# Input projections by one level of Strassen's identity, with output projections in a phase of their own

## The chip, the cores and the metric

One core of one Trainium2 chip runs the whole inference step in one launch. The metric is device microseconds of that core. The core has five engines with their own instruction streams: TensorE (PE) for matmuls, VectorE (DVE), ScalarE (ACT), GpSimd (POOL) and SyncE (SP); DMA transfers are issued from SP's, ACT's and POOL's queues. Matmuls read from on-chip memory (SBUF, 128 partitions) and write to PSUM, which has eight banks of 128 x 512 fp32 numbers.

## The reference

Two decoder layers on 1024 prompt rows and 64 sample rows (8 sequences of 8), all fp32. Layer 0 mixes with a gated short convolution, layer 1 with differential attention; a SwiGLU feed-forward follows each.

```python
D_MODEL, SEQ, D_FF, ALPHA = 1024, 1024, 2816, 4 ** 0.25
gb, gc, h = split(x @ w_conv_in, 3)               # layer 0, w_conv_in 1024 x 3072
u = gc * h                                        # with two rows of state ahead of it
conv = taps[0]*u[s] + taps[1]*u[s+1] + taps[2]*u[s+2]
m = (gb * conv) @ w_conv_out                      # 1024 x 1024
...                                               # layer 1: q, k, v = x @ w_qkv; rope; attention
m = attention_rows @ w_attn_out                   # 1024 x 1024
x = layernorm(ALPHA * x + m)                      # both layers, rows of prompt and samples alike
gate, up = split(x @ w_ffn_in, 2)                 # 1024 x 5632
x = layernorm(ALPHA * x + (silu(gate) * up) @ w_ffn_out)   # 2816 x 1024
```

## The kernel before

Every fp32 operand of a large matmul is split into a high and a low part (`split_to`, L74: ACT copies to the rounded type, DVE subtracts), and a product is three passes, high x high, high x low and low x high (`passes`, L87). The activations stand transposed in SBUF, features on partitions: `xTh` and `xTl`, eight blocks of 128 x 1088 columns (64 sample rows, then 1024 prompt rows).

*Input projections* (`in_type`, L98). One feature tile is 128 columns of a weight matrix. Its weights are loaded (`load_split`, one DMA of 512 KB and one split of 128x1024), and for each of three column chunks (364, 362, 362) 8 x 3 matmuls accumulate in one PSUM bank, which a callback consumes: for the convolution a copy or a product by the gate, for the feed-forward a Silu (L367) or a product (L372), whose result is split at once into `hh` and `hl`, the stationary operands of the output projection.

*Output projections* (`out_type`, L117) are mixed into the input projections: `run_chunks` makes two features (or 1, 3, 4 at the ends), then adds their part of the output to all eight row tiles of the residual stream, which stays in SBUF (`st`). For a row tile and a half of the columns 3 matmuls of 512 columns per feature accumulate in one bank, and DVE adds the bank to the stream (`residual`, L115). Sample rows take fp32 matmuls of their own (L125). In the last of these chunks each row tile gets its layer norm (`ln_prompt`, L151) and, two tiles later, its transposes into `xTh` and `xTl` (`to_xT`, L211), while other row tiles are still being multiplied.

*Attention* (layer 1) projects q, k and v in pieces of 256 columns (L687), with paged sample attention interleaved; its normalised heads are transposed and split into `xTh` and `xTl` by `place` (L803). The stream waits in DRAM (`x2_dram`) meanwhile.

The order of instructions on each engine is set by a planner that takes, of those it believes ready, the one that stands first in the program; within `manual_schedule` blocks an engine keeps the program's order. Each engine then runs its instructions in that order.

```python
wsp = ...tile_pool(name="wsp", bufs=9)            # split weights, 4 KB a partition each
pout, pin: 4 + 4 PSUM banks                       # output sums, input sums
run_chunks(pout, st, (2,) * 9 + (4,), feature, i_["wfo"][layer], ln)
```

Of the kernel before, what the change touches and what calls it, by code (L numbers as in the profile page):

```python
# [18 lines left out]
P = 128  # L19
# [5 lines left out]
CH = ((0, 364), (364, 362), (726, 362))  # L25
# [4 lines left out]
DS = 8  # L30
# [7 lines left out]
LAM_INIT = 0.8 - 0.6 * math.exp(-0.3)  # L38


class Ring:
    def __init__(self, *pools):
        self.pools = cycle(pools)

    def tile(self, *args, **kw):
        return next(self.pools).tile(*args, **kw)
# [3 lines left out]
def decoder_kernel(ctx: ExitStack, tc: tile.TileContext, i_: dict, o_: dict):  # L50
# [5 lines left out]
    wsp = ctx.enter_context(tc.tile_pool(name="wsp", bufs=9))  # L56
# [4 lines left out]
    xTh = cst.tile([P, KT, NT], F32R, name="xTh")  # L61
    xTl = cst.tile([P, KT, NT], F32R, name="xTl")
    mhalf = cst.tile([P, 1], F32, name="mhalf")
    POOL.memset(mhalf, -0.5)

    q_dram = drp.tile([NP, D], F32, name="q_dram")
    x2_dram = drp.tile([NP, D], F32, name="x2_dram")
    s2_dram = drp.tile([P, 512], F32, name="s2_dram")
    pairs = cst.tile([P, P], F32, name="pairs")
# [28 lines left out]
    def in_type(pin, src, consume, chunks=CH):  # L98
        wh, wl, _ = src if isinstance(src, tuple) else load_split(src)
        for c0, cw in chunks:  # L100
            ps = pin.tile([P, 512], F32, name="pin", tag="pin")
            for k in range(KT):
                for n, (a, b) in enumerate(passes(wh, wl, xTh, xTl)):
                    PE.matmul(  # L104
                        ps[:, :cw], a[:, k * P:(k + 1) * P], b[:, k, c0:c0 + cw],
                        start=(k == 0 and n == 0), stop=(k == KT - 1 and n == 2),
                    )
            consume(c0, cw, ps[:, :cw])

    def residual(a, ps, first, s):  # L110
        if first or s is not None:
            kw = {} if s is None else {"accum_out": s}
            DVE.scalar_tensor_tensor(a, a, ALPHA if first else 1.0, ps, op0=ALU.mult, op1=ALU.add, **kw)
        else:
            DVE.tensor_tensor(a, a, ps, op=ALU.add)  # L115

    def out_type(pout, st, acts, wts, first, ln=None, at=0):  # L117
        last = len(acts) - 1

        def sample():  # L120
            ss = sml.tile([P, 1], F32, name="lsms", tag="lsms", bufs=2) if ln else None
            ps = pout.tile([P, 512], F32, name="pouts", tag="pout")
            for j, ((_, _, hs), (_, _, raw)) in enumerate(zip(acts, wts)):
                for half in range(2):
                    PE.matmul(ps[half * NS:half * NS + NS, :], hs, raw[:, half * 512:half * 512 + 512],  # L125
                              start=(j == 0), stop=(j == last), skip_group_check=True)
            residual(st["s"], ps, first, ss)
            return ln_sample(pout, st, ss, ln) if ln else iter(())

        for t in range(8):  # L130
            if t == at:
                side = sample()
            t0 = NS + t * P
            s = sml.tile([P, 2], F32, name="lsm", tag="lsm") if ln else None
            for hf in range(2):
                ps = pout.tile([P, 512], F32, name="pout", tag="pout")
                cs = slice(hf * 512, hf * 512 + 512)
                for j, ((ah, al, _), (wh, wl, _)) in enumerate(zip(acts, wts)):
                    for n, (a, b) in enumerate(passes(ah, al, wh, wl)):
                        PE.matmul(ps, a[:, t0:t0 + P], b[:, cs],  # L140
                                  start=(j == 0 and n == 0), stop=(j == last and n == 2))
                residual(st[t][:, cs], ps, first, None if s is None else s[:, hf:hf + 1])
            if ln:
                ln_prompt(st, t, s, ln)
                next(side, None)
                if t >= 2 and ln["turn"]:
                    to_xT(pout, st[t - 2], t - 2)
        if ln and ln["turn"]:
            to_xT(pout, st[6], 6)
            to_xT(pout, st[7], 7)  # L150

    def ln_prompt(st, t, s, ln):
        x = st[t]
        g, b = ln["gb"]
        nmu = sml.tile([P, 1], F32, name="nmu", tag="nmu")
        DVE.tensor_scalar(nmu, s[:, 0:1], s[:, 1:2], -1.0 / D, op0=ALU.add, op1=ALU.mult)
        junk = ln["pool"].tile([P, D], F32, name="junk", tag="gb", bufs=1)
        ss = sml.tile([P, 1], F32, name="lss", tag="lss")
        ACT.activation(junk, x, AF.Square, bias=nmu[:, 0:1], accum_out=ss)
        r = rstd_of(ss, 1.0 / D, EPS)  # L160
        if t == 7 and not ln["turn"]:
            y = st[0]
            DVE.scalar_tensor_tensor(y, x, nmu[:, 0:1], g, op0=ALU.add, op1=ALU.mult)
            for eng, cs in ((SP, slice(0, 512)), (ACT, slice(512, D))):
                DVE.scalar_tensor_tensor(y[:, cs], y[:, cs], r[:, 0:1], b[:, cs], op0=ALU.mult, op1=ALU.add)
                eng.dma_start(ln["keep"][t * P:t * P + P, cs], y[:, cs])
            return
        DVE.scalar_tensor_tensor(x, x, nmu[:, 0:1], g, op0=ALU.add, op1=ALU.mult)
        DVE.scalar_tensor_tensor(x, x, r[:, 0:1], b, op0=ALU.mult, op1=ALU.add)
        if ln["keep"] is not None:  # L170
            SP.dma_start(ln["keep"][t * P:t * P + P, :], x)

    def ln_sample(pout, st, s, ln):
        x = st["s"]
# [7 lines left out]
        ps = pout.tile([P, 1], F32, name="pln", tag="pout")  # L182
        PE.matmul(ps, pairs, s, start=True, stop=True)
        nmu = sml.tile([P, 1], F32, name="nmus", tag="nmus", bufs=2)
        DVE.tensor_scalar(nmu, ps, -1.0 / D, None, op0=ALU.mult)
        junk = ln["pool"].tile([P, D], F32, name="junk", tag="gb", bufs=1)
        ss = sml.tile([P, 1], F32, name="lsss", tag="lsss", bufs=2)
        ACT.activation(junk[:, :512], x, AF.Square, bias=nmu[:, 0:1], accum_out=ss)
        yield
        ps = pout.tile([P, 1], F32, name="pln", tag="pout")  # L190
        PE.matmul(ps, pairs, ss, start=True, stop=True)
        t = sml.tile([P, 1], F32, name="lts", tag="lts", bufs=2)
        DVE.tensor_copy(t, ps)
# [6 lines left out]
        ln["keeps"](x)  # L200
        if ln["turn"]:
            ps = pout.tile([P, 4, 2, NS], F32, name="ptrs", tag="pout")
            for j in range(4):
                PE.transpose(ps[:, j, :, :].rearrange("p h t -> p (h t)"), x[:, j * P:j * P + P], ident)
            hi, lo = (y[:, :, 0:NS].rearrange("p (h j) t -> p j h t", j=4) for y in (xTh, xTl))
            ACT.copy(hi, ps)
            DVE.tensor_tensor(lo, ps, fv(hi), op=ALU.subtract)
            if ln["turn"] == "f32":
                DVE.tensor_copy(xsT.rearrange("p (h j) t -> p j h t", j=4), ps)

    def to_xT(pout, x, t):  # L211
        cs = slice(NS + t * P, NS + t * P + P)
# [743 lines left out]
```

## Time and profile before

| | |
|---|---|
| median of 3 runs | 2844.37 us (2843.62 to 2847.08) |
| profiled execution: span | 2845.2 us (the profile gives no time beside it) |
| busy: PE, PEld, DVE, ACT, POOL | 99%, 87%, 42%, 25%, 9% |
| bytes moved by DMA | 307.5 MB, 108 GB/s over the span |
| instructions | 45546 |

From the chain in order of time the stages are: convolution, about 0 to 407 us; feed-forward of layer 0, to 1213; attention, to 1950; attention output and second feed-forward, to the end. A view by groups gives busy time, mean time of one instruction, and the idle time ahead with what ended it; "PEld" is TensorE loading its stationary operand, which overlaps its matmuls. A matmul's own time in such a row is from start to finish and overlaps the next one's, so that the rate is read from a run of them in the chain. A view by stretches gives, for each stretch, the busy time and count of PE, PEld, DVE, ACT and POOL, TensorE's granted clock (1 is full speed), the share of the DMA engines and GB/s.

### The profile page before, as it was taken

What the parts mean: (1) busy time and instruction counts of PE and PEld (TensorE: products, weight loads), DVE (VectorE), ACT (ScalarE), POOL (GpSimd) and SP (SyncE); (2) the same over time, 40 slices, a digit from 0 to 9 for tenths busy, and PEclk for the clock granted to TensorE, in tenths of its full rate; (3) what the DMA queues carried; (4) which work ended last, traced back from release to release, by engine and by line L of the source; (5) the groups of instructions that cost most, each with busy time, mean ns of one, the idle gap of its engine ahead of it and who ended that gap; (6) DMA issues with size and microseconds to landing.
All of it is one profiled execution on the core that took longest, in us unless ns stands there. A gap on an engine that the chain in (4) does not pass through costs nothing.

```text
span 2845.2 us, 45546 instructions
## 1 busy us (share of the span) xinstructions
PE 2810.5 (99%) x19092; PEld 2474.1 (87%) x19092; DVE 1190.4 (42%) x2083; ACT 704.7 (25%) x1366; POOL 253.7 (9%) x517
## 2 busy tenths in 40 slices
PE   9999999999999999999999999999999999999998
PEld 9998989999999999879888666667799999999996
DVE  4435373333333332722222566676733333333325
ACT  3111141111111111312221455562311111111111
POOL 0000020000000000311111223231200000000002
PEclk9999999999999999999999999999999999999999
DMA  6111021111111111486777888761211111111102
GB/s 225 39 39 57 25 83 42 44 43 44 45 43 45 45 44 31 137 284 205 268 273 259 290 275 297 275 211 60 75 52 45 45 45 45 45 45 45 45 30 78
DMA packets 87456, 307.50 MB, mean 108 GB/s; under 512 B 10929, under 2 KB 11586, under 8 KB 87250
## 3 DMA queue, kind: packets, MB, share of 16 engines
q1 hardware_dynamic: 76194, 265.45, 27.7%
q0 software_dynamic: 10624, 38.35, 4.1%
q8 instruction: 150, 2.46, 0.4%
q10 hardware_dynamic: 432, 0.79, 0.1%
q14 instruction: 56, 0.46, 0.0%
HBM read 282.46 MB, written 22.09 MB: 107 GB/s over the span
## 4 chain that ended last, share of the span: by engine, by line
PE 93%; DMA 2%; DVE 1%; POOL 1%; ACT 1%; issue 1%; SPq 0%; POOLq 0%; DVEq 0%; ACTq 0%
PE pin L104 46%; PE pout L140 21%; PE psqkv L687 9%; PE psS L752 3%; PE psO L590 3%; PE pso L787 2%; PE psS L532 2%; PE pouts L125 2%; PE psaT L780 1%; PE psq L474 1%; DMA vpg<-cv 1%; PE psS L755 1%; POOL rs_t L93 1%; PE pstr L726 0%; PE ptr L216 0%
## 5 line engine op out<-in xcount | busy, mean ns | idle before, releaser
L104 PE MATMUL pin<-xTh,whi 128*128 128x362 f32 (+1 forms) x2688 | 876.0, 326 | 6.4 <-ACT xTh L75 6.4
L104 PE MATMUL pin<-xTl,whi 128*128 128x362 f32 (+1 forms) x2688 | 875.6, 326 | 0.3 <-DVE xTl L76 0.3
L104 PE MATMUL pin<-xTh,wlo 128*128 128x362 f32 (+1 forms) x2688 | 875.0, 326 | 0.0
L76 DVE TENSOR_TENSOR wlo<-raw,whi 128x1024 fp32r<-128x1024 f32 (+1 forms) x197 | 239.9, 1218 | 687.9 <-PE pin L104 400.7
L104 PEld LDWEIGHTS pin<-xTh,whi 128*128 128x128 f32 x2688 | 505.6, 188 | 7.4 <-ACT xTh L75 6.4
L104 PEld LDWEIGHTS pin<-xTl,whi 128*128 128x128 f32 x2688 | 505.6, 188 | 1.6 <-DVE xTl L76 0.7
L104 PEld LDWEIGHTS pin<-xTh,wlo 128*128 128x128 f32 x2688 | 505.6, 188 | 0.1
L75 ACT CAST whi<-raw 128x1024 fp32r<-128x1024 f32 (+1 forms) x197 | 203.8, 1045 | 729.7 <-PE pout L140 379.0
L140 PE MATMUL pout<-whi,hh 128*128 128x512 f32 x704 | 279.3, 397 | 0.0
L140 PE MATMUL pout<-whi,hl 128*128 128x512 f32 x704 | 278.6, 396 | 0.0
L140 PE MATMUL pout<-wlo,hh 128*128 128x512 f32 x704 | 278.0, 395 | 0.0
L687 PE MATMUL psqkv<-whi,xTh 128*128 128x256 f32 x768 | 222.5, 290 | 0.0
L687 PE MATMUL psqkv<-wlo,xTh 128*128 128x256 f32 x768 | 214.5, 279 | 0.0
L687 PE MATMUL psqkv<-whi,xTl 128*128 128x256 f32 x768 | 214.4, 279 | 0.0
L140 PEld LDWEIGHTS pout<-whi,hh 128*128 128x128 f32 x704 | 132.6, 188 | 45.7 <-issue 14.6
L140 PEld LDWEIGHTS pout<-whi,hl 128*128 128x128 f32 x704 | 132.7, 189 | 31.2 <-issue 1.6
L367 ACT ACTIVATE sg<-pin 128x364 f32<-128x364 f32 x132 | 62.6, 474 | 388.6 <-PE pin L104 388.6
L140 PEld LDWEIGHTS pout<-wlo,hh 128*128 128x128 f32 x704 | 132.6, 188 | 30.1
L687 PEld LDWEIGHTS psqkv<-whi,xTh 128*128 128x128 f32 x768 | 144.5, 188 | 15.6 <-issue 14.5
L372 DVE TENSOR_TENSOR hf<-pin,sg 128x364 f32<-128x364 f32 x132 | 70.4, 533 | 207.0 <-PE pin L104 207.0
L115 DVE TENSOR_TENSOR acc<-acc,pout 128x512 f32<-128x512 f32 x160 | 109.3, 687 | 93.5 <-PE pout L140 93.5
L687 PEld LDWEIGHTS psqkv<-wlo,xTh 128*128 128x128 f32 x768 | 144.7, 188 | 0.0
(216 smaller groups left out, 3236.7 us busy)
## 6 DMA issues: line engine op xcount, KB each, us to landing
kpg<-ck SPq DMA_DIRECT2D x128, 512.0 KB, 5.6
vpg<-cv SPq DMA_DIRECT2D x128, 512.0 KB, 5.0
raw<-wfi SPq DMA_DIRECT2D x88, 512.0 KB, 4.0
raw<-wfo SPq DMA_DIRECT2D x44, 512.0 KB, 3.7
raw<-wqkv POOLq DMA_DIRECT2D x24, 512.0 KB, 5.6
raws<-wqkv SPq DMA_DIRECT2D x24, 512.0 KB, 6.4
raw<-wci SPq DMA_DIRECT2D x23, 512.0 KB, 3.7
acc<-xn SPq DMA_DIRECT2D x8, 512.0 KB, 9.7
```

The lines of the kernel that those rows point to most:

```text
L75: ACT.copy(hi, src)
L76: (eng or DVE).tensor_tensor(lo, src, fv(hi), op=ALU.subtract)
L104: PE.matmul(ps[:, :cw], a[:, k * P:(k + 1) * P], b[:, k, c0:c0 + cw], start=(k == 0 and n == 0), stop=(k == KT - 1 and n == 2),)
L115: DVE.tensor_tensor(a, a, ps, op=ALU.add)
L125: PE.matmul(ps[half * NS:half * NS + NS, :], hs, raw[:, half * 512:half * 512 + 512], start=(j == 0), stop=(j == last), skip_group_check=True)
L140: PE.matmul(ps, a[:, t0:t0 + P], b[:, cs], start=(j == 0 and n == 0), stop=(j == last and n == 2))
L367: ACT.activation(sg[:, c0:c0 + cw], ps, AF.Silu)
L372: DVE.tensor_tensor(hf[:, :cw], ps, sg[:, cs], op=ALU.mult)
L532: PE.matmul(ps[32 * t:32 * t + 32, n, :], qp[:, 2 * t + h2, :], kp[:, 2 * t + h2, :], start=(h2 == 0), stop=(h2 == 1), skip_group_check=True)
L590: PE.matmul(O[32 * t:32 * t + 32, :], PT[:, p, 32 * t:32 * t + 32], vp[:, 2 * t:2 * t + 2, :].rearrange("p h d -> p (h d)"), start=(p == 0 ...
L687: PE.matmul(ps[t][:, t % 2, :256], a[:, k, t0:t0 + P], b_[:, cs], start=(k == 0 and n == 0), stop=(k == KT - 1 and n == 2), skip_group_che ...
L752: PE.matmul(svs[c][:, bk, :], a[cp, i, :], b_[cp, bk * w:bk * w + w], start=(m == 0), stop=(m == 2), skip_group_check=True)
```

## The change

1. *Strassen in the input projections.* Two feature tiles (A1, A2) by the 1024-deep contraction in two halves of 4 blocks, and the 1088 columns in two halves of 544 (each 32 sample rows and 512 prompt rows), make a 2 x 2 by 2 x 2 block product. It is formed from 7 block products in place of 8. `Combos` holds seven activation operands, each of 4 blocks x 544 columns, split high and low (B11, B21, B22 and the combinations X1 to X4). `Weights.make` forms the weight operand of a product: a half of a tile as loaded, or a difference or sum of halves (DVE), then split.
2. `in_type` runs the products in a written order, two chunks of 272 columns each, 12 matmuls a chunk. PSUM is four buffers of two banks. Product 6, then 5, then 3 accumulate on product 1's buffer, with a copy to SBUF taken in between; product 4 accumulates on product 7's. ACT copies and DVE adds put the four output blocks together.
3. Outputs of the input phase go to DRAM (`z_dram`, `h_dram`), not split.
4. *Separate output phase.* `out_type` takes row tiles in three groups, (0, 1, 4), (2, 5, 6), (3, 7), and for each group runs over all features (8 or 22), accumulating the whole contraction in PSUM. For each group and feature it loads and splits the weights again, and loads and splits the group's rows. Layer norm follows each group. Three `x` buffers hold residual rows.
5. After convolution and attention output, `Combos.pair` transposes row tiles t and t + 4 and forms the seven operands; after layer 0's feed-forward `to_plain` fills `xTh` and `xTl`, which live only until attention ends. Attention's `place` writes heads to `a_dram` through POOL's queue.
6. At the start the host's transposed input is loaded in blocks and the operands formed by chunk. `wsp` has 8 buffers for 9; the stream lies in DRAM (`x_dram`).

```diff
-CH = ((0, 364), (364, 362), (726, 362))
+CH = ((0, 32), (32, 32), (64, 240), (304, 272), (576, 240), (816, 272))
+HALF = NT // 2
+CW = HALF // 2
+GROUPS = ((0, 1, 4), (2, 5, 6), (3, 7))
...
+        def pair(self, psum, x1, x2, q):
+            cs = slice(32 + q * P, 32 + q * P + P)
...
+            ps = turned(0)
+            t1, t3 = scratch("t1"), scratch("t3")
+            self.put(B11, cs, v(ps[:, 0, :]))
+            ACT.copy(t3, ps[:, 1, :])
+            DVE.tensor_tensor(t1, t3, ps[:, 0, :], op=ALU.subtract)
+            ps = turned(4)
+            t2 = scratch("t2")
+            DVE.tensor_tensor(t2, ps[:, 1, :], t1, op=ALU.subtract)
+            DVE.tensor_tensor(t3, ps[:, 1, :], t3, op=ALU.subtract)
+            self.put(B21, cs, ps.rearrange("p n (k t) -> p n k t", k=4), 2)
+            self.put(X1, cs, v(t1))
+            self.put(X3, cs, v(t3))
+            t4 = scratch("t4")
+            DVE.tensor_tensor(t4, ps[:, 0, :], t2, op=ALU.subtract)
+            self.put(X2, cs, v(t2))
+            self.put(X4, cs, v(t4))
...
+    class Weights:
...
+            elif p == 6:
+                self.s1, self.s4 = scratch("s1"), scratch("s2")
+                DVE.tensor_tensor(self.s1, half(1, 0), half(1, 1), op=ALU.add)
+                DVE.tensor_tensor(self.s4, self.s1, half(0, 0), op=ALU.subtract)
+                src = self.s4
...
+            w = wsp.tile([P, 2, 512], F32R, name="ws", tag="w")
+            split_to(w[:, 0, :], w[:, 1, :], src)
...
+    def in_type(psum, x, work):
+        order = [(0, 1), (0, 2)]
+        for n in range(len(work)):
+            order += [(n, 7), (n, 6)] + ([(n + 1, 1)] if n + 1 < len(work) else []) + [(n, 5)]
+            order += ([(n + 1, 2)] if n + 1 < len(work) else []) + [(n, 4), (n, 3)]
...
+        prep(6)
+        with tc.manual_schedule(engines={mybir.EngineType.PE}):
+            for at, (n, p) in enumerate(order):
+                put = work[n][1]
+                w = made.pop((n, p))
+                if p in (1, 2, 7):
+                    banks[n, p] = psum.tile([P, 2, 512], F32, name=f"pin{p}", tag="b")
+                ps = banks[n, {1: 1, 6: 1, 5: 1, 3: 1, 7: 7, 4: 7, 2: 2}[p]]
+                mm(ps, w, p, p in (1, 2, 7))
+                v = ps[:, :, :CW]
+                if p in (1, 6, 5):
+                    ACT.copy(put.dst({1: 0, 6: 2, 5: 3}[p]), v)
+                if p in (2, 5, 4):
+                    blk = {2: 0, 5: 3, 4: 2}[p]
+                    d = put.dst(blk)
+                    DVE.tensor_tensor(d, d, banks[n, 7][:, :, :CW] if p == 5 else v, op=ALU.add)
+                    put.done(blk)
+                elif p == 3:
+                    put.last(v)
+                prep(at + 7)
...
+    def out_type(psum, pool, nf, h_src, s_src, w_src, res, res_s, ln):
+        gb = [pool.tile([P, D], F32, name=f"ln{nm}", tag=f"ln{nm}", bufs=1) for nm in "gb"]
+        for t, nm in zip(gb, ("ln_g", "ln_b")):
+            SP.dma_start(t, i_[nm][ln["n"]:ln["n"] + 1, :].partition_broadcast(P))
...
+                w = load_split(w_src[f])
+                raw = pool.tile([P, len(ts), P], F32, name="hr", tag="hr", bufs=2)
...
+                hh = pool.tile([P, len(ts), P], F32R, name="hh", tag="hh", bufs=2)
+                hl = pool.tile([P, len(ts), P], F32R, name="hl", tag="hl", bufs=2)
+                split_to(hh, hl, raw)
...
+        prep(2)
+        for g, ts in enumerate(GROUPS):
+            pss = [psum.tile([P, 2, 512], F32, name="pout", tag="b") for _ in ts]
...
+            for t in ts:
+                kept[t] = pool.tile([P, D], F32, name="x", tag="x", bufs=3)
+                SP.dma_start(kept[t], res(t))
+            for f in range(nf):
+                (wh, wl, raw), hh, hl, hs = made.pop((g, f))
+                for n, ps in enumerate(pss):
+                    for hf in range(2):
+                        cs = slice(hf * 512, hf * 512 + 512)
+                        for m, (a, b) in enumerate(passes(hh[:, n, :], hl[:, n, :], wh[:, cs], wl[:, cs])):
+                            PE.matmul(ps[:, hf, :], a, b, start=(f == 0 and m == 0), stop=(f == nf - 1 and m == 2))
...
+                prep(g * nf + f + 3)
+                if f >= 2 and side:
+                    side.pop(0)()
+            while side:
+                side.pop(0)()
...
+            for n, t in enumerate(ts):
+                ln_prompt(kept[t], pss[n], t, gb, ln)
+            for t in ts:
+                side += [lambda th=th: th() for th in ln["turn"](t, kept)]
...
+    def ln_prompt(x, ps, t, gb, ln):
+        for hf in range(2):
+            DVE.scalar_tensor_tensor(x[:, cs], x[:, cs], ALPHA, ps[:, hf, :], op0=ALU.mult, op1=ALU.add,
+                                     accum_out=s[:, hf:hf + 1])
...
+        ACT.activation(ps.rearrange("p a b -> p (a b)"), x, AF.Square, bias=nmu[:, 0:1], accum_out=ss)
...
-            ACT.activation(xTh[:, h, cs], pv, AF.Copy, scale=gs[:, 0:1])
-            DVE.scalar_tensor_tensor(xTl[:, h, cs], pv, gs[:, 0:1], fv(xTh[:, h, cs]), op0=ALU.mult, op1=ALU.subtract)
+            oT = ap2.tile([P, 512], F32, name="oT", tag="oT", bufs=1)
+            ACT.activation(oT, ps.rearrange("p a b -> p (a b)"), AF.Copy, scale=gs[:, 0:1])
+            POOL.dma_start(a_dram[h][:, t0:t0 + 512], oT)
```

More of the change, by code (lines that the diff above doesn't have):

```diff
@@ L38 @@
 LAM_INIT = 0.8 - 0.6 * math.exp(-0.3)
[L41 to L46, printed above, removed]
+GROUPS = ((0, 1, 4), (2, 5, 6), (3, 7))
+B11, B21, B22, X1, X3, X2, X4 = range(7)
 @with_exitstack
@@ L96, in rstd_of @@
         return r
[L98 to L150, printed above, removed]
```

578 lines of the change are left out of this document (371 added, 207 removed).

## The prediction

> **What bounds the kernel now.** I read the busy shares first, then the chain that ended last by line, then that chain in order of time, then groups, stretches and DMA issues.
>
> ```profile
> PE 2810.5 (99%) x19092; PEld 2474.1 (87%) x19092; DVE 1190.4 (42%) x2083; ACT 704.7 (25%) x1366; POOL 253.7 (9%) x517
> PE 93%; DMA 2%; DVE 1%; POOL 1%; ACT 1%; issue 1%; SPq 0%; POOLq 0%; DVEq 0%; ACTq 0%
> by line: PE pin L104 46.0%; PE pout L140 21.4%; PE psqkv L687 9.5%; PE psS L752 2.8%; PE psO L590 2.6%; PE pso L787 2.3%; PE psS L532 2.2%; PE pouts L125 1.7%; PE psaT L780 1.3%; issue 0.9%; PE psq L474 0.9%; DMA vpg<-cv 0.6%; PE psS L755 0
> ```
>
> TensorE is the chain. 46.0% of 2845.2 us, 1309 us, is the input projections (L104), the part that Strassen shrinks. A matmul's mean in the groups is a latency with overlap, so I take the pitch from runs of the chain:
>
> ```profile
> 7.31 108.37 PE pin L104 x647
> 494.96 46.75 PE pin L104 x288
> 543.57 22.68 PE pout L140 x96
> 684.29 1.87 PE pouts L125 x8
> 1184.57 0.87 PE ptr L216 x8
> 1271.60 5.81 PE psqkv L687 x48
> 1277.98 3.01 PE psqkv L687 x24
> 407.00:1136.00 729.00, 729.00 (x4067) 674.69 (x4068) 247.74 (x349) 124.71 (x193) 5.20 (x22) 1.00 0.14 45
> 356.00:407.00 51.00, 49.16 (x259) 41.19 (x258) 45.32 (x79) 24.49 (x40) 16.38 (x21) 1.00 0.21 67
> ```
>
> At 362.7 columns (mean) the pitch is 46.75/288 = 162.3 ns; 8064 of them are 1309 us, as the chain says. At 512 it is 22.68/96 = 236 ns. At 256, 24 more matmuls cost 5.81 - 3.01 = 2.80 us: 116.7 ns. In a stretch (the columns: length, busy PE, PEld, DVE, ACT, POOL, clock, DMA share, GB/s) the feed-forward has no idle TensorE at all, and the seam after the convolution's last sum, with DVE 45 of 51 us busy, only 1.8 us. So the seams that the change adds are not there yet.
>
> **The change, part by part.** The profiled span is 2845.2 us, nothing is known around it, and the median of the runs is 2844.4; I sum against 2845.2.
>
> *Fewer columns.* A pair of feature tiles took 2 x 72 matmuls of 362.7 columns; now 7 products x 2 chunks x 4 x 3 = 168 of 272. 56 pairs (12 conv, 44 feed-forward) make 9408. Pitch at 272 between the rows: 116.7 + 16 x 45.6/106.7 = 123.5 ns, so 1162 us: -147. Bounds: scaled from 256, 124.0 ns (-142); from 362.7, 121.7 ns (-164).
>
> *New input-phase work beside it.* A pair lasts 168 x 123.5 ns = 20.7 us on TensorE.
>
> ```profile
> L76 DVE TENSOR_TENSOR wlo<-raw,whi 128x1024 fp32r<-128x1024 f32 (+1 forms) x197 | 239.9, 1218 | 687.9 <-PE pin L104 400.7
> L76 DVE TENSOR_TENSOR hl<-hf,hh 128x362 fp32r<-128x362 f32 x88 | 47.1, 536 | 39.4 <-ACT hh L75 39.4
> L115 DVE TENSOR_TENSOR acc<-acc,pout 128x512 f32<-128x512 f32 x160 | 109.3, 687 | 93.5 <-PE pout L140 93.5
> L693 ACT COPY nat<-psqkv 128x512 f32<-128x512 f32 x48 | 28.1, 585 | 184.1 <-PE psqkv L687 173.4 <-issue 6.5 <-DMA raw<-wqkv 4.0
> L323 DVE SCALAR_TENSOR_TENSOR gc<-u,taps,gc 128x1024 f32<-128x1024 f32 x16 | 20.6, 1285 | 0.6
> ```
>
> DVE goes as 0.16 us + 1.03 ns an element. Feed-forward pair: 7 splits and 4 weight combinations of 512 (0.69), 5 block operations of 544 (0.72) = 11.2 us, 54%; ACT, with some 12 operations of 0.6, 7 us. Conv adds three taps (1.29 each): near 75%. Throughput hides it. What can surface is a handover: product 5 must not overwrite bank A before ACT has copied 6 out, and 4 not bank C before ACT and DVE have read it; each is covered by one product, 24 x 0.1235 = 2.96 us, against 0.6 + 0.72 us and one operation ahead on each queue (0.6 + 0.69): 2.6 us. It just fits; where a 1.29 us tap lies ahead it doesn't. Bounds 0 and 90 us (56 x 1.6); I take +10, near the fit. The products' outputs go out by DMA, no longer through splits; weights come by prefetch of six products, hidden.
>
> *Start.* Before: 7.31 + 108.37 - 647 x 0.1623 = 10.7 us lost. Now the inputs become seven operands per chunk: 7 splits + 4 differences of 1088 (1.28) = 14 us of DVE for each of two chunks, and the first weights' splits come behind them in program order. With data at 5.5 us DVE is through them at 33.5; by then the first two products can have run, 6 us: 27.5 lost, +17. Bounds +5, +25.
>
> *Output phase.* Matmuls are the same 2880 of 512 columns and the same sample pieces. The weights are loaded and split three times (180 for 60), rows come back from DRAM.
>
> ```profile
> raw<-wfo SPq DMA_DIRECT2D x44, 512.0 KB, 3.7
> kpg<-ck SPq DMA_DIRECT2D x128, 512.0 KB, 5.6
> acq<-x_dram SPq DMA_DIRECT2D x8, 512.0 KB, 4.8
> lng<-ln_g SPq DMA_DIRECT2D x4, 512.0 KB, 4.5
> x_dram<-acc SPq DMA_DIRECT2D x8, 512.0 KB, 2.7
> 1213.00:1583.00 370.00, 367.59 (x3960) 322.24 (x3960) 89.42 (x326) 77.57 (x142) 46.95 (x101) 1.00 0.77 258
> 1945.00:1950.00 5.00, 2.72 (x14) 1.58 (x11) 1.64 (x3) 1.07 (x3) 3.60 (x7) 1.00 0.00 2
> 1950.00:1955.00 5.00, 4.78 (x15) 3.82 (x16) 1.74 (x3) 0.69 (x1) 0.17 (x1) 0.66 0.00 0
> 2821.01 0.23 DVE nmu L156
> 2821.34 1.25 ACT junk L159 x2
> 2822.67 1.29 POOL rs_t L93
> 2824.03 0.56 POOL rs_r L95
> 2824.61 1.28 DVE acq L169
> ```
>
> A step with three row tiles is 18 x 0.236 = 4.25 us (+0.94 for the samples, 1.87 us for two features), with two 2.83 us. DVE splits cost 1.22 + 0.56 us of it: hidden. In the last group a step moves 640 KB in 2.83 us, 230 GB/s: under the 258 that attention sustains, but three weight buffers, each held for a landing of 3.7 to 5.6 us and a split, turn in 8.5 us, and three steps are 8.5 us. Over 44 feed-forward steps: 0 to +40; I take +10.
>
> *Into the output phase.* hr, hh and hl lie on the input phase's memory, so SP's row loads wait for its last matmul, behind the two norm vectors (4.5 us); then a split of 1.1 us. About 6.5 us at each feed-forward (before: 0). Conv: the last z must also land (2.7 us), 7. Attention: the same 6.5, of which 2.3 idle were there before (the stretch 1945 to 1950): +4. Together +24; bounds 0 (other memory) and +35.
>
> *Out of conv and attention output.* Three x buffers serve eight rows, and pair needs t and t+4. pair(0) stands behind the second group's last matmul, T. Two sets of transposes (0.87 each) with evacuation between them: T+4. Only then may x for t=2 and 5 load: T+9. LN releases the next bank at T+12, so the third group, 22.6 us, ends at T+33 or later. Row 6 waits for pair(1), row 7 for pair(2): T+44; its LN (residual 1.4, then the rows above, 4.8) T+50; transposes and first split T+52. TensorE had 22.6 + 7 us of work: 22 us lost, 2 of them there already (the 356 to 407 row). DVE alone needs much the same: after T four pairs at 7.4 us, LN of five rows at 4.2, splits 8: 59 us (a pair is 11 operations near 0.69, LN 2 x 0.69 + 0.23 + 2 x 1.28), of which the last 7 may trail. +42 for both. Bounds: 0, if the planner puts pair(0) earlier, and +80.
>
> *Other ends.* The second layer's attention and the kernel's end each wait for two rows' LN instead of one: +3 each. Attention now stores its rows with 16 DMAs on POOL's queue in place of a DVE subtraction each; POOL, 9% busy, hides the issues: 0, and if the last store is waited for, +3 (its landing, as the 2.7 of x_dram).
>
> *Clock.* TensorE's granted clock falls after a wait: 0.66 in the stretch from 1950, after 2.3 us idle, and
>
> ```profile
> 1205.00:1210.00 5.00, 3.60 (x31) 3.40 (x30) 3.04 (x19) 1.94 (x3) 0.00 (x0) 1.00 0.94 253
> 1210.00:1215.00 5.00, 2.10 (x10) 1.14 (x12) 0.56 (x4) 0.13 (x1) 0.80 (x1) 0.86 1.03 407
> 1215.00:1220.00 5.00, 5.00 (x34) 3.62 (x30) 0.00 (x0) 0.00 (x0) 0.00 (x0) 0.80 1.00 360
> ```
>
> The first cost 5 x 0.34 = 1.7 us; the second, 1.4 + 2.9 us idle, cost 5 x (0.14 + 0.20) = 1.7. I count ten new ones above (start, three entries, three at each of two exits), 1.4 each: +14; bounds 0 and +17. The Trainium skill, "TensorE: Matmul & The Clock Gate", section "What's actually happening", says that an idle window of about 3.4 us halves the clock until some 3.4 us of work have passed; by that rule ten gaps would cost an estimated 17 us. The trace agrees in kind (0.66).
>
> The Trainium skill's same page, section "LDWEIGHTS (loading the stationary operand)", gives P/1.2 ns for a weight load, an estimated 107 ns for 128 columns: by it a 272-column matmul (113 ns at full clock) isn't load-bound, and the saving stands as summed. The 116.7 ns of the 256-column row agrees.
>
> **Sum:** -147 + 10 + 17 + 10 + 24 + 42 + 6 + 14 = -24: 2821 us.
>
> **Rivals.** *The seams overlap.* If the planner turns pair(0) early and prefetches rows, exits cost 10, entries 8, handovers 0, clock 5: -147 + 17 + 10 + 10 + 8 + 6 + 5 = -91, 2754 us. For it: before, the planner hid LN and transposes down to 1.8 us. Against: the three x buffers are a true dependence.
>
> *Handovers stall every pair (the other side).* DVE and ACT take instructions in order, and any second one ahead of the copies adds 0.6 to 1.3 us past the 0.4 us left. At 1.2 us in each of 56 pairs it is 67 us where I took 10: +33, 2878 us. It decides above 0.61 us a pair, 34/56. For it: the 2.6 of 2.96 us; against: nine other operations spread over 20.7 us, one engine 54% busy.
>
> *The last group is DMA-bound.* Steps of 3.8 us instead of 2.83 on 44: 43 instead of 10, 2854 us, no change to a little slower. For it: three buffers; against: raw's 3.7 us when the queue is light.
>
> *Matmuls don't shrink in proportion.* The change then doesn't do what it says: at 139 ns 9408 are 1309, and with the seams 2968 us. Against: the 116.7 ns row, same weights' shape.
>
> **How the numbers follow.** Forecast 0.57 (2775 to 2843), seams overlap 0.17, handovers 0.13, DMA-bound 0.11, no shrinking 0.02. The prediction is the forecast's 2821. The range, 2765 to 2875, takes in the forecast, half of the overlap case, the DMA case and half of the handovers (up to 1.1 us a pair): 0.83. A change within 0.2% (2839 to 2850) is what this kernel's runs can't tell from none: a tenth of the forecast and a third of the DMA case, 0.09. Faster: the rest of the forecast, the overlap case and a third of the DMA case, 0.72; slower: what is left, 0.19.
>
> **What would show it.** Right: runs of pin at 123 to 124 ns a matmul, 24 in 2.96 us, with no idle TensorE inside the feed-forward's input stretch; pout unchanged at 236; idle TensorE of 20 us around pair in both mixers' outputs, released by x loads and DVE; 5 to 8 us at each entry, released by hr's DMA; clock under 1.00 behind them. Wrong: waits of pin on ACT or DVE in each pair (handover), hh waiting for raw's DMA in the last groups, or exits under 10 us.

## The result, and the profile after

| | before | after |
|---|---|---|
| median | 2844.5 us (2843.6 to 2847.1) | 2909.3 us (2906.8 to 2913.8), 4 runs |
| ratio | 1 | 1.0226, 95% interval 1.0211 to 1.0240 |
| profiled span | 2845.2 us | 2905.6 us |
| TensorE busy, idle | 2810.5, 34.7 us | 2728.5, 177.1 us |
| granted clock, mean | 0.998 | 0.971 |
| moved by DMA | 307.5 MB | 455.0 MB |

The change is slower, and lies 34 us above the upper end of the predicted range. By the spans TensorE's busy time fell by 82.0 us and its idle time rose by 142.4: +60.4.

The page's busy shares, and the chain in order of time (start, length, what):

```profile
PE 2728.5 (94%) x20436; PEld 2364.7 (81%) x20436; DVE 1497.9 (52%) x2565; ACT 1043.0 (36%) x1921; POOL 253.4 (9%) x481
...
33.70 243.61 PE pin L240 x1918
453.98 450.01 PE pin L240 x3574
926.57 6.90 PE pout L321 x18
934.48 4.34 PE pout L321 x18
1093.05 49.47 PE pout L321 x216
```

The input phases are unbroken runs of matmuls, 693.6 us for 5492: 126.3 ns each where 123.5 were forecast. The output's 512-column matmul is unchanged or a little better (49.47/216 = 229 ns). The first output step behind an entry takes 6.90 us where the next takes 4.34: its first 12 matmuls start 0.43 us apart, at half clock, the rest 0.23.

What ended TensorE's waits (engine and line waited for: us in all, times, longest):

```profile
PE pout L321 <- ACT hh L76: 43.6, 6, 10.9
PE ptr L124 <- DVE x L363: 21.0, 4, 8.2
PE pin L240 <- ACT ws L76: 18.6, 3, 17.0
PE pin L240 <- DVE ws L77: 12.1, 4, 8.5
PE ptr L414 <- DVE x L363: 11.3, 3, 6.4
PE pout L321 <- DVE t L146: 10.1, 2, 5.0
PE ptr L124 <- DVE t L137: 9.4, 4, 4.3
```

Nearly all of it is at seams: `hh` is (but for some 4 us) an entry into an output phase, `ws` is mostly the start, `ptr` and `t` are the exits, L414 is the transposes ahead of attention. In stretches (length, busy PE, PEld, DVE, ACT, POOL, clock, DMA share, GB/s):

```profile
0.00:27.00 27.00, 5.82 (x26) 5.28 (x26) 17.93 (x16) 13.55 (x15) 0.29 (x5) 1.00 0.76 231
281.00:302.00 21.00, 8.12 (x52) 7.69 (x50) 4.75 (x6) 1.12 (x2) 0.00 (x0) 0.72 0.38 132
382.00:440.00 58.00, 36.27 (x167) 28.83 (x165) 51.58 (x89) 29.46 (x51) 7.31 (x9) 0.80 0.48 160
454.00:918.00 464.00, 461.10 (x3646) 460.44 (x3646) 236.82 (x349) 156.19 (x264) 0.00 (x0) 1.00 0.22 76
917.00:927.00 10.00, 1.24 (x8) 1.02 (x7) 1.18 (x2) 1.13 (x2) 0.00 (x0) 0.74 0.71 225
1143.00:1207.00 64.00, 62.48 (x283) 50.83 (x282) 44.57 (x59) 34.00 (x49) 5.98 (x9) 1.00 0.73 227
1207.00:1230.00 23.00, 9.84 (x48) 8.59 (x47) 13.42 (x20) 8.38 (x10) 6.45 (x10) 0.63 0.60 181
1965.00:1986.00 21.00, 6.96 (x25) 4.89 (x25) 1.14 (x3) 3.81 (x9) 4.89 (x9) 0.50 0.40 125
2065.00:2124.00 59.00, 37.26 (x169) 29.35 (x168) 51.01 (x89) 29.79 (x53) 8.87 (x9) 0.83 0.48 164
```

The reader is to see two kinds of row. Inside a phase (454 to 918, and the last group, 1143 to 1207) TensorE is busy at full clock. At a seam it works an eighth to two thirds of the time and, but for the start, at a clock of 0.50 to 0.83. At the two exits (382 to 440, 2065 to 2124) VectorE is the busy engine.

### The profile page after: what moved, and what is told of

It is laid out like the page before. It is cut to its first block, busy times and chain, and to the rows that moved or that the text cites. A ratio compares the mean times of both kernels' runs of the same rounds, so it can differ in the third digit from the quotient of the medians.

```text
span 2905.6 us, 51121 instructions
## 1 busy us (share of the span) xinstructions
PE 2728.5 (94%) x20436; PEld 2364.7 (81%) x20436; DVE 1497.9 (52%) x2565; ACT 1043.0 (36%) x1921; POOL 253.4 (9%) x481
## 4 chain that ended last, share of the span: by engine, by line
PE 64%; issue 23%; DMA 5%; DVE 3%; ACT 2%; POOL 2%; SPq 1%; DVEq 0%; POOLq 0%; ACTq 0%
PE pin L240 25%; PE pout L321 14%; PE psqkv L930 10%; PE psS L995 3%; PE psO L833 3%; PE pso L1030 2%; PE psS L775 2%; PE psaT L1023 1%; PE pouts L324 1%; DMA raw<-wfo 1%; PE psq L717 1%; DMA hr<-h_dram 1%; DVE wlo L77 1%; PE psS L998 1%; DVE xl L77 0%
## 5 line engine op out<-in xcount | busy, mean ns | idle before, releaser
L240 PE MATMUL pin<-xh,ws 128*128 128x272 f32 x6272 | 1199.4, 290 | 39.6 <-ACT ws L76 18.6
L240 PEld LDWEIGHTS pin<-xh,ws 128*128 128x128 f32 x6272 | 1000.3, 190 | 43.4 <-ACT ws L76 19.1
L240 PE MATMUL pin<-xl,ws 128*128 128x272 f32 x3136 | 914.2, 292 | 2.2 <-DVE xl L77 2.1
L240 PEld LDWEIGHTS pin<-xl,ws 128*128 128x128 f32 x3136 | 594.6, 190 | 3.1 <-DVE xl L77 3.1
L321 PE MATMUL pout<-whi,hh 128*128 128x512 f32 x960 | 391.4, 409 | 56.6 <-ACT hh L76 43.6
L77 DVE TENSOR_TENSOR wlo<-raw,whi 128x1024 fp32r<-128x1024 f32 x204 | 250.8, 1230 | 291.0 <-ACT whi L76 260.7
L76 ACT CAST whi<-raw 128x1024 fp32r<-128x1024 f32 x204 | 213.6, 1048 | 287.7 <-DMA raw<-wfo 145.6
L77 DVE TENSOR_TENSOR ws<-s,ws 128x512 fp32r<-128x512 f32 x224 | 154.5, 690 | 141.6 <-ACT ws L76 141.0
L76 ACT CAST ws<-s 128x512 fp32r<-128x512 f32 x224 | 138.8, 620 | 205.8 <-PE pin L240 103.8
L77 DVE TENSOR_TENSOR ws<-raw,ws 128x512 fp32r<-128x512 f32 x168 | 115.4, 688 | 99.6 <-ACT ws L76 99.6
```

What stands on the lines that cost most here:

```text
L76: ACT.copy(hi, src)
L77: (eng or DVE).tensor_tensor(lo, src, fv(hi), op=ALU.subtract)
L240: PE.matmul(ps[:, c, :CW], a, y, start=(start and k == 0 and m == 0), stop=(k == 3 and m == 2), skip_group_check=True)
L321: PE.matmul(ps[:, hf, :], a, b, start=(f == 0 and m == 0), stop=(f == nf - 1 and m == 2))
```

## The experiments

Ratios are to the kernel before, run beside each; the change itself stands at 1.0226 (1.0211 to 1.0240), and a version with only a dead tile added (below) at 1.0204, so a few us either way are not told apart.

**e1_store: sample rows' stores on another queue.** First theory: SP's queue stalls behind the sample rows' stores.

```diff
-        fold(ln["keeps"], lambda half: x[half * NS:half * NS + NS, :])
+        fold(ln["keeps"], lambda half: x[half * NS:half * NS + NS, :], eng=POOL)
```

> The two stores of the normed sample rows go out on POOL's queue instead of SP's; nothing else changes. Theory 1: in each of the four output phases SP stands still behind this store, which waits for POOL's last operation on xs, and the weight and row loads of the second group stand behind it; the chain of the changed kernel shows it at 369 to 380 us and at 1069 to 1083 us. With the store elsewhere the second group runs at its 4.3 us a step: about 8 us less in each phase and some clock, 2909 to 2870..2885 us. Rival (the weight buffer that holds the sample rows' norm vectors until the same POOL operation): two buffers are left for the weights either way, 2900..2909 us. Rival (the output phase is bound by its bytes, not by a wait): 2905..2909 us.

Measured 2909.2 us, 1.0216 (1.0197 to 1.0235): nothing. This theory falls.

**e1b_gbf: the sample norm's vectors from the tiles already loaded,** so that no weight buffer is held for them.

```diff
-        gb = rawp.tile([P, 2, 512], F32, name="gbf", tag="raw")
...
+                POOL.tensor_tensor(x[hs], x[hs], gb[m][hs, half * 512:half * 512 + 512], op=op)
```

> The sample rows' norm vectors are read from the two norm tiles that are there anyway (four POOL operations on half of the partitions for two), so that no weight buffer is held for them; the stores stay on SP's queue. Theory 1 (SP's queue behind the store): little, 2900..2912 us, or a little slower because POOL's chain ahead of the store is two operations longer. Rival (the held weight buffer): about 8 us less in each of four phases, 2870..2885 us.

Measured 2914.0 us, 1.0230 (1.0212 to 1.0247): nothing either. Taken singly, neither the queue nor the weight buffer sets the time.

**e2_pairs: pairs of rows handed over ahead of the sample rows.**

```diff
-                side += [lambda it=it: next(it, None)] * 5
+                samples = [lambda it=it: next(it, None)] * 5
...
+            if g == 0:
+                side += samples
```

> In the second group of each output phase the row tiles' transposes (pair, to_plain) stand ahead of the sample rows' norm in the program instead of behind it, so pair(0) comes at step 2 of the second group and frees two x buffers some 20 us earlier. Theory 1: what is lost at the end of the convolution's and attention's output (32 to 37 us each over TensorE's work) is mostly the chain pair -> x load -> norm -> pair over three x buffers; it starts earlier, and each loses 10 to 15 us less, with a few us of clock: 2875..2890 us. Rival (DVE's work after the second group sets the end): 2900..2909 us. Rival (the sample rows' chain, moved back, takes its place at the end): 2905..2920 us.

Measured 2898.4 us, 1.0167 (1.0144 to 1.0190), 10 to 17 us off where the theory had 19 to 34. From the convolution's last input matmul to the feed-forward's first it went from 146.2 to 142.3 us, from the first matmul of attention's output to the second feed-forward's first from 136.8 to 128.9. One long gap stays at each exit. VectorE in order of time, attention's exit (start, length, line, operation; in brackets idle before):

```profile
2101.20 0.68 DVE L352 SCALAR_TENSOR_TENSOR x<-x,pout 128x512 f32<-128x512 f32 x1
...
2106.56 1.28 DVE L359 SCALAR_TENSOR_TENSOR x<-x,nmu,lng 128x1024 f32<-128x1024 f32 x1
...
2109.56 0.21 DVE L355 TENSOR_SCALAR nmu<-lsm 128x1 f32<-128x1 f32 x1
2111.12 1.29 DVE L359 SCALAR_TENSOR_TENSOR x<-x,nmu,lng 128x1024 f32<-128x1024 f32 x1 [0.76 <-ACT pout L357]
```

The last row's residual is done at 2101.9, but its mean, a 0.21 us operation, waits until 2109.6 behind the pair before it in VectorE's queue; the rest of the norm, the transposes and the splits follow from there.

**e3_rows: the row buffers of the output phase in memory of their own.**

```diff
-                raw = pool.tile([P, len(ts), P], F32, name="hr", tag="hr", bufs=2)
+                raw = rowp[0].tile([P, len(ts), P], F32, name="hr", tag="hr", bufs=2)
...                                                  # hh and hl likewise
+            rowp[0] = scs.enter_context(tc.tile_pool(name="rows0", bufs=2, side="right", reuse_waits="tile"))
```

> hr, hh and hl get memory of their own instead of the input phase's, so the first rows of an output phase can be loaded and split while the input phase still runs. Theory 1: TensorE's four waits on hh at the entries (10.9, 8.8, 10.5 and 9.5 us) go at the two feed-forwards, and with them the low clock behind each (about 3 us): 2909 to 2880..2890 us. Rival (SP's loads stand behind the norm vectors' or the last store's wait in its queue and come late anyway): 2900..2909 us.

Measured 2894.6 us, 1.0157 (1.0140 to 1.0174), 13 to 20 us off. The stretch at the first feed-forward's entry, and the wait:

```profile
917.00:927.00 10.00, 10.00 (x56) 8.61 (x55) 3.29 (x5) 1.66 (x3) 0.56 (x2) 1.00 0.60 181
...
PE pout L321 <- ACT hh L76: 25.6, 4, 10.6
```

Both feed-forward entries are gone (idle 8.8 and 9.5 us before the edit), and the half clock with them. The convolution's and attention's stay, at 10.6 and 10.4: their memory comes free only when the phase before has ended. TensorE's idle time fell by 18.6 us, but the span by 10.9, for the output's matmul became dearer:

```profile
1085.72 53.85 PE pout L321 x231
```

That is 233 ns where it was 229; over 2880 matmuls 11 us are lost again. The four runs with this edit (e3_rows, e9_entries, e11_all, e15_best) show 233, the other versions of the changed kernel 229. Why isn't known.

**e4_widths: seven widths in one kernel.**

```diff
-                        PE.matmul(ps[:, c, :CW], a, y, ...
+                        w_ = CW if start and k == 0 and m == 0 else WID[p]
+                        PE.matmul(ps[:, c, :w_], a, y[:, :w_], ...
```

> Each of the seven products gets its own width, 272, 270, 268, 266, 264, 258 and 256 columns; the sums of the columns left out are missing, so this is a kernel for the pitch alone. Theory width (a streamed matmul costs a fixed part and so much for each column): the pitch falls on one line from 126 ns at 272 to 117 ns at 256, about 0.55 ns for each column, so 121.6 at 264 and 118 at 258. Rival step (a width costs more when it falls in a certain class, as 364 columns cost 167 ns and 362 only 160 in the kernel before): the pitch falls by about 6 ns at once between two neighbours, with 270, 266 and 258 on the one side or 272, 264 and 256 on the other.

From start to start in the input projections at full clock, means over 1,200 to 1,500 matmuls each:

```text
columns   256    258    264    266    268    270    272
ns       118.7  120.3  121.5  122.7  123.3  124.9  126.0
```

No step of 6 ns: 0.2 to 0.8 ns a column from one width to the next, 0.46 on average, and 126.0 at 272 again. Attention's projection, 256 columns too, costs 116.6 in this run: the same width is 2 ns cheaper there. (One run, 2872.7 us.)

**e5_warm: filler matmuls to keep the clock.**

```diff
+                for _ in range(34):
+                    PE.matmul(pq[:, 1, 0:P], ident, ident, start=True, stop=True, skip_group_check=True)
...                                                  # and 24 ahead of the last pairs
```

> 34 small matmuls into an unused bank at the entry of each output phase and 24 ahead of the last groups of handing over at the two long exits keep TensorE at work while it waits. Theory clock: the first steps after an entry take 6.9 us instead of 4.3 because the clock is granted at a half there; with the filler the first step takes about 4.4 us, the half-clock stretches at the entries go, and the time falls by 10 to 20 us, to 2889 to 2899. Rival rows: the first steps are long because their normed rows arrive one by one; then the granted clock rises but the steps stay long and the time stays within 4 us of 2909.

Measured 2907.4 us, 1.0207 (1.0190 to 1.0224): no gain that can be told. The mean clock rose from 0.971 to 0.981, the time at half clock fell from 170 to 112 us by the clock's records. The entry in the chain:

```profile
925.27 1.94 PE pouts L326 x2
927.22 6.31 PE pout L323 x18
933.53 1.00 PE pouts L326 x2
934.53 4.34 PE pout L323 x18
...
PE pouts L326 <- DMA hs<-h_dram: 8.6, 2, 4.5
```

The filler didn't do what it was for. At the feed-forward's entry it ran in the first 4 us behind the last product, TensorE then stood idle for another 4 us until the sample rows had landed, two of their matmuls came first, and the first step began 10.6 us behind the last product where it had been 8.8, its first ten matmuls still at half clock. The convolution's entry and the second feed-forward's look alike. At attention's entry the first step does run at full clock, but starts nearly 5 us later. So neither theory is settled by the time. That the first steps are long by the clock, and not by rows that come one by one, is in the even 0.43 us between their matmuls; what a clock kept at full would give back stays open.

**e8_start: first halves first.**

```diff
+            for c in (0, 1):
+                for n, p in order[:3]:
...
+                    mm(banks[n, p], made[n, p], p, True, (c,))
```

> The first three products of each input phase run all their first 272 columns before their second 272. Theory start: at the start and after the two long exits TensorE waits for the rows of the second half, and the first half of the next products would have been ready; the three places give back 1.5 to 3 us each, 2901 to 2905 in all. Rival: what is late is the first half and the weights themselves, so the time stays within 3 us of 2909.

Measured 2919.2 us, 1.0262 (1.0245 to 1.0279), slower by 10 to 16 us. Both theories miss; the start still waits 11 us, for the weights' splits, which stand behind the second half of the rows on VectorE. Each input phase takes 4 to 5 us longer; why stays open.

**e6_plain: eight plain products in the same layout.**

```diff
-        order = [(0, 1), (0, 2)]
+        order = [(n, t, k) for n in range(len(work)) for t in (0, 1) for k in (0, 1)]
...
+                    for k, b in enumerate(((B11, B21), (X1, B22))[h]):
+                        mm(ps, made[n, t, k], b, k == 0)
```

> The four output blocks are made with the eight plain products instead of Strassen's seven; layout, phases, staging and evacuations stay, the forming of the combined rows too. Theory: the input phases are bound by TensorE, so 1344 more matmuls at 126 ns add 169 us and the time is about 3078. Rival (VectorE's forming of weight combinations and its additions to the row store set the pace of the phases, so that the seven products were not free to run at their pitch): the plain form adds clearly less, under 120 us.

Measured 3062.0 us, 1.0758 (1.0736 to 1.0779). A whole feed-forward phase is one row of the chain:

```profile
474.16 532.69 PE pin L237 x4211
```

That is 126.5 ns a matmul. The layout with its seams costs 215 us when the products stay eight, some 51 of them because the matmuls are narrower (10752 at 126.5 ns are 1360 us, where 1309 did the same work before); seven products for eight give 153 of them back, nine tenths of 1344 x 126 ns = 169. The identity does what it says. All other stages together changed by under 5 us (3059.6 - 2905.6 = 154.0 by the spans, 149.3 of it in the three input phases).

**e9_entries: entries and pairs together,** with the first step's rows in scratch slots and the norm vectors behind them.

```diff
+        if first:
+            return scp.tile([P, 512], dt, name=name, tag="sc")[:, 0:n * P].rearrange("p (n t) -> p n t", t=P)
...                                                  # and the two edits above
         prep(2)
+        for t, nm in zip(gb, ("ln_g", "ln_b")):
```

> The two edits that gained (pairs of rows handed over ahead of the sample rows, and a place of their own for the normed rows of an output phase) together, and the entries of the conv and attention output eased too: the first step's rows go into the scratch slots that the input phase has already given back, and the norm vectors are asked for behind the first two steps' rows. Theory entries and exits (the waits at the seams are what the change lost; each that is taken away comes back in full): the two edits add up to 37 us, the conv and attention entries give another 8 to 16, so 1.003 to 1.007 of the time before. Rival (a wait taken away at a seam only moves to the next one, the exits being set by VectorE): the two edits overlap and the time stays above 1.012.

Measured 2876.7 us, 1.0098 (1.0080 to 1.0116): 30 to 36 us off, half of the loss, between the two theories. The convolution's entry, attention's, and both exits:

```profile
280.00:310.00 30.00, 23.46 (x106) 16.49 (x105) 8.36 (x12) 4.14 (x6) 0.00 (x0) 0.84 0.59 199
373.00:430.00 57.00, 40.66 (x173) 32.41 (x172) 45.90 (x82) 26.79 (x49) 8.36 (x11) 0.82 0.51 167
1956.00:1966.00 10.00, 1.39 (x4) 0.90 (x4) 0.56 (x1) 1.56 (x3) 1.44 (x3) 0.50 0.36 111
2043.00:2105.00 62.00, 42.14 (x209) 32.88 (x207) 52.70 (x91) 31.65 (x56) 10.11 (x12) 0.92 0.49 164
```

The convolution's output now starts right behind its last product (12 of the first step's 18 matmuls have no record in this trace). Its third step starts 17.6 us behind that product, where it was 22.7 in e3_rows and is 10.6 at this run's feed-forward entries: the rows of the steps behind the first are late next. Attention's entry is hardly better, and the exits are still 16 to 20 us idle each.

**e11_all: the next phase's first products ahead of the last pair,** the weights' splits ahead too, also at the start.

```diff
+            if last and ln.get("begin"):
+                ln["begin"].run()                   # chunk 0 of products 1 and 2
...
+                    if ch:
+                        begun.make()
```

> The same, and at the two long exits the first half of the next phase's first two products (24 matmuls, 3 us) is put ahead of the last pair of rows, with their weights split ahead of the last norm; at the start of the kernel the first two products' weights are split ahead of the second half of the rows. Theory: 3 us for each exit and about 4 us at the start on top of the run before, so 0.999 to 1.004 of the time before. Rival: the weights' splits delay the last norm on VectorE by as much as TensorE gains, so the two runs agree within 0.1%.

Measured 2877.7 us, 1.0099 (1.0080 to 1.0117): the same as the run before, the time that the rival gave. The products start 10 and 6.5 us earlier, and the input phases end within 3 us of where they did. Whether the norm's delay is the reason isn't shown: at the second exit the last two rows' transposes start 3.4 us later than before, at the first exit one pair's 1.5 later and the other's 2.8 earlier.

**e10_order: the kernel before with its chunks in another order.**

```diff
-CH = ((0, 364), (364, 362), (726, 362))
+CH = ((0, 362), (362, 364), (726, 362))
```

> The kernel before with its three column chunks as 362, 364, 362 instead of 364, 362, 362. Theory width (364 columns cost 167 ns and 362 cost 160 because of their count): the second chunk now takes 167 and the first 160. Rival place (the first chunk is slow for where its columns stand): the first chunk stays at 167 or near it though it has 362 columns, and the second at 160.

Measured once, 2867.8 us beside 2847.7. In the chain:

```profile
499.68 47.84 PE pin L104 x288
```

166.1 ns a matmul instead of 162.3. Start to start in the first feed-forward: 163.5, 168.2 and 166.6 ns for the chunks in order, where the kernel before had 166.7, 160.0 and 160.3. Neither theory: the last chunk has the same columns in the same place in both and costs 160 or 167.

**e12_align: every tile 32 bytes further.**

```diff
+    cst.tile([P, 8], F32, name="pad")
```

> The changed kernel with one unused tile of 32 bytes for each partition ahead of its others, so that every tile behind it stands 32 bytes further: the streamed rows start at multiples of 64 bytes where they started 32 bytes past one. Theory place (the pitch of a matmul depends on where its operands stand, not on their width alone, as the same 362 columns cost 160 ns in one order of the chunks and 164 to 167 in another): the pitch of 272 columns moves by some ns, at most to 120, which would give 9408 x 6 ns = 56 us back. Rival (the pitch goes by width, or by what VectorE, ScalarE and the transfers do meanwhile): the pitch stays within 1 ns of 126 and the time within 5 us of 2909.

Measured 2906.3 us, 1.0204 (1.0187 to 1.0221); the pitch stays at 125.9 ns. The place by 32 bytes is not it.

**e13_xpool and e15_best: two of seven splits of each pair on GpSimd,** in the changed kernel and in the eased one.

```diff
-            self.put(X1, cs, v(t1))
+            self.put(X1, cs, v(t1), eng=POOL)
...                                                  # X4 likewise
```

> At the exits of the conv and attention output GpSimd makes the low parts of two of the seven operands of each pair of rows (X1 and X4, the last that the next phase needs): two operations of 512 less for VectorE in each pair, four pairs, 0.68 us each, 5.5 us an exit. Theory VectorE (it is busy 52 of 59 us at the conv exit and 52 of 62 at the other, and its chain sets when the next phase starts): 8 to 11 us come back, 2898 to 2901. Rival (the loads of the rows into three buffers, or the norm's own latency, set the end): less than 3 us.

> The version that eased the entries and the order of the pairs, with the same move to GpSimd. Theory VectorE: 8 to 11 us off 2876.7, so 2866 to 2869. Rival (there the last norm's latency ends the exits, one long gap of 8.5 and 10.9 us behind the last output matmul): within 3 us of 2877.

Measured 2906.8 us, 1.0207 (1.0188 to 1.0225), and 2876.6 us, 1.0100 (1.0083 to 1.0117): nothing in either. The convolution's exit, after and with the move:

```profile
381.00:440.00 59.00, 37.27 (x172) 29.65 (x170) 51.82 (x89) 30.46 (x53) 7.31 (x9) 0.80 0.48 163
```

```profile
381.00:440.00 59.00, 38.88 (x165) 30.69 (x164) 48.51 (x83) 28.81 (x50) 17.12 (x15) 0.78 0.46 157
```

VectorE is 3.3 us freer and the exit no shorter. The last row's mean, with which the closing chain begins, shows why (after, then with the move):

```profile
437.16 0.21 DVE L353 TENSOR_SCALAR nmu<-lsm 128x1 f32<-128x1 f32 x1
...
436.91 0.20 DVE L353 TENSOR_SCALAR nmu<-lsm 128x1 f32<-128x1 f32 x1
```

In both versions VectorE is busy almost without a break for the 10 us ahead of it, with the last pairs and norms, so the work taken off brought the mean only 0.25 us forward. This doesn't clear VectorE: it shows that an exit isn't set by the sum of its work alone, but also by a chain through the engines (rows loaded into a freed buffer, residual, mean, square on ScalarE, two small operations on GpSimd, norm, transposes, splits) and by where its short links stand in VectorE's queue, which the pairs' order moved by 4 and 8 us. Three row buffers hold this chain's head; more of them weren't tried. How much each link is worth stays open.

## Why the prediction was wrong

TensorE's busy time was to fall by the matmuls less the clock, 133 us, and fell by 82; its idle time was to rise by 109 and rose by 142. By the prediction's terms, after less before:

| term | predicted | measured | from |
|---|---|---|---|
| 9408 matmuls of 272 | -147 | -121 | 126.3 ns in the chain |
| clock | +14 | +35 | starts of matmuls in half-clock stretches, 37.5 us over full pitch against 2.4 |
| start | +17 | +17 | first matmul at 17.0, then gaps of 2.3 and 8.5; before 10.7, of it 6.6 idle |
| handovers | +10 | +6 | 2.0 us at the end of each of three input phases |
| last group, DMA | +10 | 0 | TensorE busy 62.5 of its 64 us |
| entries | +24 | +37 | gaps of 10.9, 8.8, 10.5 (2.3 before) and 9.5 |
| exits of both mixers | +42 | +51 | idle 27.0 and 27.0 (381 to 454, 2064 to 2142); 1.8 and 1.5 before |
| other ends | +6 | +12 | 13.2 ahead of attention (4.3 before), +3 at the end |
| not in the sum | | +23 | 19 of idle time, 12 of it in gaps under 0.9 us; 4 of busy time |
| sum | -24 | +60 | spans: +60.4 |

**The matmul's size** was the first step to fail. The straight line between a 256- and a 362-column pitch gave 123.5, with bounds of 121.7 and 124.0; the measured 126 is outside them. e4_widths shows where it went wrong: 256 columns in the input projections cost 118.7, and the line began at 116.7, read from attention's projection, which still costs 116.6 there. That is 2 of the 2.5 ns; the rise of 0.46 ns a column is close to the line's 0.43. By e10_order the line's upper end, 162.3 at 362.7 columns, isn't that width's price either: in another order of the chunks it was 166.1. The bounds took the pitch in one place for a law; what it is about the place stays open.

**The clock** was the second, +21. Ten gaps of 1.4 us were counted; the records show 18 stretches at half clock, 3.4 to 27.3 us long. The step took each wait alone, and at a seam waits follow each other: at the convolution's exit one stretch at half clock, 13.7 us from 385.8, spans two waits of 4.3 and 5.0 us with 1.9 us of work between. The Trainium skill, "TensorE: Matmul & The Clock Gate", section "HAM oscillation — how this bites in real kernels", describes just that for a loop of short work and waits of 3 to 5 us; the 0.50 of the stretch from 1965 agrees. e5_warm took a third of the half-clock time away and gained nothing that can be told, but there the first steps also started later; what this term would give back stays open.

**The entries** failed by +13, past their bound of 35. The mechanism is the predicted one, shown by e3_rows: with memory of their own the rows' loads are early and the feed-forward's entries vanish. The size was short: 8.8 to 10.9 us where 6.5 to 7 were taken, and attention's, set at +4, was +8.

**The exits** were inside their bounds, 51 for 42, and the chain of pair, load, norm and transposes was the right place: by e2_pairs its order counts, by e1_store SP's queue behind the stores doesn't. How far VectorE's load sets it isn't settled. **The start** (+17) and the kernel's end (+3) came as computed, the handovers and the last group better; ahead of attention +9 came for +3. Another 23 us are in no term, half of them short gaps.

Of the rivals, *handovers stall every pair* falls by the stretch from 454 to 918, 461 of 464 us busy; *the last group is DMA-bound* by 1143 to 1207; *no shrinking* by the pitch, 126.3 ns where it needed 139. *The seams overlap* is true only of a kernel with other memory and order, and there only in part (e9_entries, 1.0098, with 11 us given away by the output's dearer matmul). What happened was none of them: the forecast's own terms, where they missed, missed mostly upwards. The range was built from single mechanisms, each with the other terms at their middle; five small terms estimated from the same idea (a wait costs its own length) share their error, and no case held that.

## What to carry to other kernels

An engine at 99% is kept there by overlap, and a change that saves work on it by separating phases pays at every seam a chain of latencies through the other engines. Price the layout alone first (here the same phases with the old arithmetic: +215 us against 153 saved), and give the next phase's first operands memory of their own and an early place in the queues; here that and the order of handing over returned half of the loss. When a sum has many small terms of one kind, let them be wrong together in the range.

## What the runs showed of the hardware

- The distance between two matmuls with a fresh stationary operand each is not a function of the columns alone: 362 columns cost 160.0 to 166.7 ns in two orders of the same chunks, 20 us over the kernel, with the last chunk unmoved; 256 cost 118.7 in the input projections and 116.6 in attention's, in one run; 512 cost 229, and 233 once the output's rows had memory of their own. 272 cost 125.9 on average in five versions, in a pattern of 121 to 132 ns that repeats every 24. Moving every tile by 32 bytes changed neither the pattern nor its mean. The cause is open.
- TensorE's granted clock stayed at 0.5 for 27.3 us around attention's end, where it had worked 7.0 of 21 us. Raising the mean clock from 0.971 to 0.981 with idle matmuls moved the time by nothing that can be measured; of the first steps behind the entries only attention's ran at full clock by it.
